# A smaller descriptor area for indirect transfers, and one more raw and one more split weight buffer, in a recurrent block with 32 experts

## The chip, the core and the metric

The kernel runs on one core of a Trainium2 chip. The metric is the device time of one launch in microseconds (us), as the median of several runs. A core has five engines with instruction queues of their own, each worked through strictly in order: PE (TensorE, matmuls; its weight loads are listed as PEld), DVE (VectorE), ACT (ScalarE), POOL (GpSimd) and SP (SyncE). They meet only through semaphores. Data moves between the large memory (HBM) and the on-chip memory (SBUF, 128 partitions) by transfers on 16 DMA engines. SP issues the plain transfers; POOL issues the indirect ones, whose rows are picked by an index, and the descriptors of those lie in SBUF.

## The reference: what is computed

One layer over 2048 tokens of width 1024: a gated linear recurrence with a short convolution, a layer norm, a mixture of 32 experts of which each token takes two, and a second layer norm. The part that matters here is the mixture. Cut down, with the names of the reference:

```
expert = g_idx[:, None] * EXPERTS_PER_GROUP + top_i      # two of 32 for each token
...
def expert_block(args):
    xb, e = args
    hdn = jax.nn.silu(xb @ w1[e]) * (xb @ w3[e])          # 1024 -> 512, twice
    return hdn @ w2[e]                                    # 512 -> 1024
...
out = jnp.einsum('tk,tkd->td', gates.astype(x.dtype), y_slots)
```

`w1`, `w3` and `w2` are float32, 32 experts with 3 matrices of 1024 x 512 numbers each: 201 MB that have to be read once, whatever the tokens choose.

## The kernel before, in words

**Two stages.** The first, up to about 740 us, is the recurrence (`Recurrence`), which routes each token as it goes. The second runs the experts one after the other in the order of a table, and behind them, sixteen tiles of 128 tokens at a time, the last layer norm.

**Weights.** PE multiplies in float16, so each float32 weight is split into a high and a low float16 half, and products take three passes. The 32 experts' weights come in 384 loads (12 for each expert: 4 of `w1`, 4 of `w3`, 4 of `w2`) of 128 x 1024 float32 numbers, 512 KB. Each passes through these steps:

- SP issues the load into a buffer `raw` (`load_raw`, L1286). A raw buffer takes 4 KB of each partition.
- ACT writes the high half (`split_hi`, L1300) into a buffer `w`, and DVE then writes the low half (`split_lo`, L1304). For a few early loads POOL does the latter (L1644) after another ACT step (L1640). With that, the raw buffer is free again.
- A buffer `w` holds both halves of two loads, 8 KB of each partition. PE reads it in the up matmuls (`up`, L1415) or the down matmuls (`down`, L1442, and L1358 for tokens beyond 128). When the last of these is done, the buffer is free.

There are `RAWS` = 6 raw buffers and `RING` = 10 buffers `w`. Two of the weights' buffers, once, lie in a place that is otherwise used by the last layer norm (`SPARE`).

**Tokens.** POOL gathers the expert's tokens (L1315, `exs<-xhl` and `rxT<-xhl`, and `sxg<-xhl` for those beyond 128), PE transposes them (L1399, L1346), ACT copies the result to `xT` (L1404, L1349). After the up matmuls come `silu` (ACT, L1420), the product (DVE, L1427) and its split (L1431 ACT, L1435 DVE). The down matmuls' result is scaled by ACT (L1448, L1365) and POOL adds it to the tokens' rows in HBM (L1307, `acc<-row` and `acc<-sxg`). The last layer norm fetches finished rows with POOL (L1315, `y<-acc`, and `w<-acc` for the last two tiles, which lie in a buffer `w`), normalizes them with DVE and ACT (L1505 to L1529) and stores them with POOL (L1307, `out<-y`, `out<-w`). The last expert's first 128 tokens skip the way through HBM: they are fetched (`row<-acc`), finished and stored (`out<-row`) in one go, and their sums are added as well (`acc<-row`).

**What sets the order.** The order on each engine is fixed when the program is built. `Plan` records every operation with its engine, an assumed duration, what it needs and which buffers it takes. `Plan.run` then plays the program once and takes, on each engine, what can start first, by due time among those that can. A buffer that isn't free holds an operation back. So the number of buffers of each kind (`slots`, here `"raw": RAWS, "w": RING` in `MOE`) goes into the order of all engines. On the chip the engines keep that order and wait on semaphores.

**Where loads stand on SP.** A first group of loads is issued while the recurrence still ends. Then the experts' order is known, and SP reads for each coming expert its number (L1573, `TENSOR_LOAD er`) and loads its list of tokens (L1387 `idx`, L1327 `sidx`): a block of six experts' lists, into which only a few weight loads are mixed.

```
r = add("raw", "SP", 0.5, load, behind=[k.early_done] + [x.op for x in regs], dma=2.91 * WQ / 2048,
        uses=[raw] + regs)
...
a = add("w_hi", "ACT", act(WQ), hi, [r], behind=[k.big_done] * spare, uses=[raw, w])
e, us, f = ("POOL", 2.3, rest_) if on_pool else ("DVE", dve(WQ), lo)
```

**SBUF.** `bacc.Bacc` sets aside a part of each partition for the descriptors of POOL's transfers; unless it is told otherwise, 16 KB.

Of the kernel before, what the change touches and what calls it, by code (L numbers as in the profile page):

```python
# [56 lines left out]
TAIL = [13, 16, 18, 19, 21, 22, 24, 25, 26, 28, 29, 30, 31, 31, 32, 32]  # L57
WQ = 1024
NQ = 4096 // WQ
RING, RAWS = 10, 6  # L60
NOV = 64
ON_POOL = range(1, 24, 3)
SPARE = (10, 11)
# [1877 lines left out]
```

## Time and profile before

| what | value |
|---|---|
| median of 3 runs | 1574.86 us (1574.77 to 1576.59) |
| time of the profiled execution | 1576.59 us |
| its span, first to last instruction | 1574.8 us |
| mean granted TensorE clock | 0.966 of full speed |
| PE busy | 1419.7 us, 90% of the span |
| DVE busy | 1200.5 us, 76% |
| ACT busy | 1079.3 us, 69% |
| POOL busy | 326.7 us, 21% |
| DMA traffic | 371.87 MB, mean 236 GB/s |

The shares are means over two stages with different limits. The rows of the profile on which an argument rests are shown in the prediction, each ahead of its use. In the rows with windows of time, the columns are the window, its length, and for each engine the busy time with the number of instructions; the last three are the granted clock, the mean busy share of the 16 DMA engines, and GB/s. In the rows of a timeline they are start, duration, engine, line, operation, `out<-in`, and in brackets the idle time ahead of it with what ended it. SPq is SP's queue, which only issues. The chain of waits follows the work that ended last back in time; its rows are start, duration and what ran or was waited for.

### The profile page before, as it was taken

The numbers are of one execution on the slowest core, as the hardware profiler recorded it, in microseconds if no ns is written. First come the engines' busy times: TensorE is split into PE (matmuls) and PEld (weight loads), VectorE is DVE, ScalarE is ACT, GpSimd is POOL, SyncE is SP. The second block draws the span as 40 slices with busy tenths as digits, with TensorE's granted clock in tenths as the row PEclk, the third lists the DMA queues.
The fourth block names the chain that finished last, engine by engine and source line by source line (L and its number), as shares of the span: only waits on it lengthen the run. The fifth ranks groups of instructions, "written<-read, shape, count | busy, mean of one in ns | idle before, by whom it ended". The sixth has DMA issues, their size and how long they took to land. (4 is left out here: it accounts for less than half of the span.)

```text
span 1574.8 us, 33932 instructions
## 1 busy us (share of the span) xinstructions
PE 1419.7 (90%) x13223; PEld 961.8 (61%) x13223; DVE 1200.5 (76%) x2118; ACT 1079.3 (69%) x1417; POOL 326.7 (21%) x382
## 2 busy tenths in 40 slices
PE   8799999999999999999788999998979789988781
PEld 3344444444444766775567788776868678767570
DVE  6799967986688757977967878876667578767784
ACT  5699545675367643775877778787677778877873
POOL 8100000000000000000543123233133133332223
PEclk9899999999999999999999999999989999999896
DMA  9476542433334433642689899999999899999994
GB/s 325 158 237 204 183 147 95 135 108 100 100 105 127 156 123 125 208 130 88 258 282 330 299 342 353 344 349 331 300 318 335 277 334 348 341 347 329 306 337 130
DMA packets 129648, 371.87 MB, mean 236 GB/s; under 512 B 28279, under 2 KB 38783, under 8 KB 129482
## 3 DMA queue, kind: packets, MB, share of 16 engines
q1 hardware_dynamic: 108554, 315.29, 56.9%
q0 software_dynamic: 20928, 54.36, 12.9%
q8 instruction: 105, 1.72, 0.4%
q14 instruction: 61, 0.50, 0.1%
HBM read 309.92 MB, written 57.53 MB: 233 GB/s over the span
## 5 line engine op out<-in xcount | busy, mean ns | idle before, releaser
L1304 DVE SCALAR_TENSOR_TENSOR w<-raw,w 128x1024 f16<-128x1024 f32 x373 | 449.2, 1233 | 125.3 <-ACT w L1300 123.2
L1300 ACT ACTIVATE w<-raw 128x1024 f16<-128x1024 f32 x380 | 389.5, 1054 | 97.9 <-DMA raw<-w 96.9
L1415 PE MATMUL h<-xT,w 128*128 128x128 f16 (+19 forms) x6528 | 421.3, 228 | 35.2 <-ACT xT L1404 13.5
L592 PE MATMUL mm<-xt,wsp 128*128 128x512 f16 (+1 forms) x2400 | 435.8, 341 | 19.0 <-ACT xt L523 6.5
L1415 PEld LDWEIGHTS <-w 128*128 128x128 f16 x6528 | 412.0, 100 | 42.6 <-DVE w L1304 19.1
L592 PEld LDWEIGHTS <-wsp 128*128 128x128 f16 x2400 | 235.8, 99 | 210.1 <-issue 16.1
L807 PE MATMUL o<-wo,y 128*128 128x512 f16 x960 | 218.5, 379 | 0.9 <-DVE wo L486 0.6
L1442 PE MATMUL o<-w,hT 128*128 128x512 f16 (+5 forms) x744 | 170.7, 384 | 9.8 <-DVE w L1304 3.4
L955 POOL DMA_INDIRECT table<-rows,dest x32 | 35.3, 1102 | 622.5 <-DVE xr L616 312.0
L807 PEld LDWEIGHTS <-y 128*128 128x128 f16 x960 | 91.8, 98 | 103.8 <-issue 1.6
L1442 PEld LDWEIGHTS <-hT 128*128 128x128 f16 (+5 forms) x768 | 81.4, 109 | 90.4 <-issue 12.4
L1307 POOL DMA_INDIRECT acc<-row,idx x32 | 61.3, 1914 | 268.7 <-ACT row L1448 233.0
L628 DVE SCALAR_TENSOR_TENSOR xc<-xr,cw,xc 128x512 f32<-128x512 f32 (+1 forms) x150 | 92.6, 640 | 2.7
L612 ACT ACTIVATE xr<-mm 128x512 f32<-128x512 f32 x40 | 23.7, 593 | 92.5 <-PE mm L592 70.3
L705 ACT ACTIVATE tg<-ri,bh 128x512 f32<-128x512 f32 (+1 forms) x100 | 58.2, 595 | 21.9 <-PE ri L700 21.1
L700 PE MATMUL ri<-xs,wg 128*128 128x512 f16 (+1 forms) x300 | 67.9, 336 | 0.3 <-ACT tg L705 0.2
L1404 ACT ACTIVATE xT<-rt 128x1024 f16<-128x1024 f16 (+5 forms) x64 | 63.9, 1002 | 4.9 <-PE rt L1399 3.9
L759 DVE TENSOR_TENSOR_SCAN th<-ta,hlast,tg 128x512 f32<-128x512 f32 (+1 forms) x50 | 52.4, 1066 | 1.4
L1448 ACT ACTIVATE row<-o,idx 128x512 f32<-128x512 f32 (+5 forms) x64 | 43.2, 677 | 14.6 <-PE o L1442 14.5
L1358 PE MATMUL o<-w,hT 128*32 128x256 f16 (+1 forms) x864 | 41.4, 307 | 13.0 <-ACT row L1448 13.0
L822 ACT ACTIVATE sd<-mv,epst 128x1 f32<-128x1 f32 x16 | 4.7, 295 | 68.1 <-DVE mv L818 57.5
L1427 DVE SCALAR_TENSOR_TENSOR hid<-h,hid 128x256 f32<-128x256 f32 (+19 forms) x68 | 30.1, 442 | 25.6 <-PE h L1415 25.4
(294 smaller groups left out, 1732.3 us busy)
## 6 DMA issues: line engine op xcount, KB each, us to landing
raw<-w SPq DMA_DIRECT2D x384, 512.0 KB
wsp<-wpre SPq DMA_DIRECT2D x80, 512.0 KB
row<-w_in SPq DMA_DIRECT2D x20, 512.0 KB
wpre<-wsp SPq DMA_DIRECT2D x20, 512.0 KB
row<-x SPq DMA_DIRECT2D x16, 512.0 KB
acc<-row SPq DMA_DIRECT2D x16, 512.0 KB
xhl<-exs SPq DMA_DIRECT2D x16, 512.0 KB
row<-w_out SPq DMA_DIRECT2D x10, 512.0 KB
```

The source lines that it names most:

```text
L592: nc.tensor.matmul(o, wt[:, a, d], x[:, b], start=(d == 0 and i == 0), stop=(d == KD - 1 and i == 2))
L628: nc.vector.scalar_tensor_tensor(xc, xr[:, t:t + N], s.cw[:, j, t:t + 1], xc, op0=OP.mult, op1=OP.add)
L700: nc.tensor.matmul(cell["ri"][j], a, b, start=(i == 0), stop=(i == len(seq) - 1))
L705: nc.scalar.activation(s.halves(c, s.tiles["t", c, js[0], g], js)[j], cell["ri"][j], AF.Tanh, scale=0.5 / WS, bias=s.bh[:, j, g:g + 1])
L759: nc.vector.tensor_tensor_scan(cut(h)[j], cut(T["a", c, q])[j], cut(t1())[j], s.hlast[:, j:j + 1], op0=OP.mult, op1=OP.add)
L807: nc.tensor.matmul(o, y[:, b, t * P:(t + 1) * P], s.wo[:, a, j, n * 512:(n + 1) * 512], start=(j == 0 and m == 0), stop=(j == NT - 1 and m ...
L1300: nc.scalar.activation(w[:, 0, o:o + WQ], raw, AF.Copy, scale=scale)
L1304: nc.vector.scalar_tensor_tensor(w[:, 1, o:o + WQ], raw, WS, w[:, 0, o:o + WQ], op0=OP.mult, op1=OP.subtract)
L1307: sc = nc.gpsimd.indirect_dma_start(out=to, out_offset=bass.IndirectOffsetOnAxis(ap=rows, axis=0), in_=y, in_offset=None, bounds_check=las ...
L1404: nc.scalar.activation(b.xT[:, a, :, :b.n], b.pt[a][:, :, :b.n], AF.Copy)
L1415: nc.tensor.matmul(ph[:, j], b.W[n, d // 4][:, a, o:o + P], b.xT[:, q, b.place[d], o0:o1], start=(d == 0 and m == 0), stop=(d == KD - 1 an ...
L1442: nc.tensor.matmul(py, k.hT[b.slot][:, a, i, :b.n], b.W["w2", i // 2][:, q, o:o + 512], start=(i == 0 and m == 0), stop=(i == KF - 1 and m ...
```

## The change

The build call gets an argument that sets the descriptors' part to 4 KB of each partition. The 12 KB that come free hold one more raw buffer (4 KB) and one more buffer `w` (8 KB).

```
-RING, RAWS = 10, 6
+RING, RAWS = 11, 7
...
-    nc = bacc.Bacc("TRN2", target_bir_lowering=False, num_devices=1)
+    nc = bacc.Bacc("TRN2", target_bir_lowering=False, num_devices=1, dynamic_dma_scratch_size=4096)
```

No instruction is added or removed, but the planner gets other numbers of buffers, and the order of all engines changes from the first weight load on. Ahead of it, in the recurrence, nothing moves. Three places.

SP, where the first weight loads stand, at the end of the recurrence (`xhl<-exs` and `acc<-row` are the recurrence's last stores):

```order
 L846 DMA xhl<-exs 128x2048
 L834 DMA acc<-row 128x1024
-L1286 DMA raw<-w 128x1024 x6
+L1286 DMA raw<-w 128x1024 x7
 L834 DMA acc<-row 128x1024
 L846 DMA xhl<-exs 128x2048
```

The first group, which needs no buffer back, is seven loads instead of six.

SP, in the block of six experts' lists. Before:

```order
L1286 DMA raw<-w 128x1024
L1327 ISA
L1327 DMA sidx<-table 128x1x4
L1573 TENSOR_LOAD er
L1573 ISA x2
L1387 ISA
L1387 DMA idx<-table 128x4
L1327 ISA
L1327 DMA sidx<-table 128x1x4
L1573 TENSOR_LOAD er
```

The same place in the change:

```order
L1286 DMA raw<-w 128x1024
L1327 ISA
L1327 DMA sidx<-table 128x1x4
L1573 TENSOR_LOAD er
L1573 ISA x2
L1387 ISA
L1387 DMA idx<-table 128x4
L1286 ISA
L1286 DMA raw<-w 128x1024
L1327 ISA
L1327 DMA sidx<-table 128x1x4
```

The first row is load 30 of before and load 31 of the change. Before, no further load stands ahead of the end of the block. In the change two more are mixed into it, so that 33 loads are issued by the end of the block where it were 30.

Behind that place the loads and splits of experts 4 to 9 stand up to five ahead of where they were, counted against the same expert's `silu` on ACT; from expert 17 on the two orders agree within two loads.

POOL, at the program's end (`row` is the last expert's tile, `w` the buffer with the last two tiles of the layer norm, `y_...` the two ahead of them; the numbers are the buffers'):

```order
 L1315 DMA row<-acc,idx 112x1024
 L1315 DMA w<-acc,tok 128x1024 x2
-L1307 DMA out<-y_20445,tok_out 2048x1024 x2
+L1307 DMA out<-y_20499,tok_out 2048x1024 x2
+L1307 DMA acc<-row,idx 2048x1024
 L1307 DMA out<-row,idx 2048x1024
-L1307 DMA out<-w,tok_out 2048x1024
-L1307 DMA acc<-row,idx 2048x1024
-L1307 DMA out<-w,tok_out 2048x1024
+L1307 DMA out<-w,tok_out 2048x1024 x2
```

The last expert's addition to HBM stood between the last two stores of the result; now it stands ahead of the last three.

## The prediction, made before the changed kernel was run

> **What bounds the kernel now.** I read the slices first, then the windows of time of the expert stage, then the waits and the chain of waits there. The slices (40 of 39.4 us each; the first row is the DMA engines' busy share in tenths):
>
> ```profile
> DMA  9476542433334433642689899999999899999994
> GB/s 325 158 237 204 183 147 95 135 108 100 100 105 127 156 123 125 208 130 88 258 282 330 299 342 353 344 349 331 300 318 335 277 334 348 341 347 329 306 337 130
> ```
>
> Up to slice 19 (750 us) the transfers have room. From slice 21 on they have hardly any. The windows say how much:
>
> ```profile
> 742.00:830.00 88.00, 71.80 (x961) 53.16 (x961) 72.58 (x159) 66.93 (x87) 39.26 (x24) 0.94 0.76 259
> 850.00:1520.00 670.00, 595.77 (x7600) 496.70 (x7601) 505.17 (x601) 510.03 (x640) 191.25 (x115) 0.96 0.97 331
> 1000.00:1100.00 100.00, 89.30 (x1167) 72.82 (x1165) 72.78 (x92) 76.62 (x99) 31.11 (x19) 0.97 1.00 350
> ```
>
> Over the 670 us from 850 to 1520 the 16 DMA engines are 97% busy, and PE is busy 596 us (89%). At a full share they move 350 GB/s. So this stage is bound by its transfers, with 3% of 670 = 20 us in which they run dry; PE is 74 us behind them, ahead of DVE and ACT. Who waits for whom, in us in total, times, and the longest:
>
> ```profile
> SPq L1286 <- DVE w L1304: 351.4, 263, 8.8
> ACT w L1300 <- DMA raw<-w: 96.9, 74, 10.0
> PE h L1415 <- DVE w L1304: 9.5, 7, 2.5
> ```
>
> SP stands 351 us in front of a weight load because the raw buffer is still held by the low split of an earlier one. That alone isn't a loss, as transfers are queued meanwhile. ACT waits 97 us for loads to land. The chain of waits goes in a circle there:
>
> ```profile
> 1390.24 10.59 DMA raw<-w
> 1400.86 1.07 ACT w L1300
> ...
> 1403.10 1.22 DVE w L1304
> 1404.35 9.99 DMA raw<-w
> 1414.36 1.06 ACT w L1300
> ```
>
> A load takes 10 to 10.6 us, mostly in the queue behind five others, then a high split of 1.07 and a low split of 1.22, and the freed buffer takes the next load. This circle of six is the place of the change.
>
> **The change part by part.** The sums are made against the profiled execution: 1576.59 us, its span 1574.8 and 1.8 around it. That execution lies 1.73 above the median of 1574.86, which I take off at the end.
>
> *Loads moved ahead: 3.* The order of SP (shown with the change) has 33 instead of 30 loads ahead of the end of the block of lists. The seventh raw buffer brings one, the eleventh buffer `w` two. In the trace that block holds the loads up:
>
> ```profile
> 816.76 0.92 SPq L1286 DMA_DIRECT2D raw<-w  x2
> 817.90 0.65 SPq L1327 DMA_DIRECT2D sidx<-table  x1
> ...
> 827.83 0.62 SPq L1327 DMA_DIRECT2D sidx<-table  x1
> 828.72 6.24 SPq L1286 DMA_DIRECT2D raw<-w  x7
> ```
>
> From 817.7 to 828.7 no load is issued, and the share between 742 and 830 is 0.76, so there is room for three more. A stage bound by transfers ends earlier by what was moved ahead of it: 3 loads of 0.524 MB at 350 GB/s, 1.50 us each, 4.5 us. The ends: nothing, if PE is what paces the stage after all, and 3 x 2.04 = 6.1 if a load's whole period counts, which is the time from the first to the last load over 383 steps:
>
> ```profile
> L1286 SPq DMA_DIRECT2D raw<-w x384: 327/333/3612, 742.7 to 1525.6; - x192
> ```
>
> I take 4.5, by the nearer row, that of the full windows.
>
> *Dry stretches.* Windows of 10 us in which the transfers run dry:
>
> ```profile
> 890.00:900.00 10.00, 10.00 (x124) 6.52 (x123) 8.62 (x11) 6.74 (x10) 3.15 (x2) 1.00 0.75 185
> 1140.00:1150.00 10.00, 2.23 (x11) 0.88 (x10) 3.06 (x5) 3.49 (x5) 0.00 (x0) 0.80 0.70 190
> 1240.00:1250.00 10.00, 6.82 (x48) 3.50 (x47) 2.77 (x3) 3.96 (x6) 0.00 (x0) 1.00 0.81 286
> 1250.00:1260.00 10.00, 5.77 (x62) 5.53 (x60) 2.88 (x5) 8.17 (x11) 2.47 (x2) 0.83 0.46 170
> 1480.00:1490.00 10.00, 7.16 (x65) 3.15 (x65) 5.26 (x6) 7.43 (x10) 2.78 (x2) 0.66 0.78 258
> ```
>
> They lack 2.5, 3.0, 1.9, 5.4 and 2.2 us, 15 of the 20. In such a stretch all loads that had a buffer have landed, and SP can't issue another. One more raw buffer puts one more load into it, 1.5 us at most: 5 x 1.5 = 7.5. Nothing shows how often the reshuffled order meets such a stretch again, so I take the middle between 0 and 7.5, 3.7 us, and keep for the range 0 and the whole 20.
>
> *The end.* The last additions and stores of POOL, and what two of them wait for:
>
> ```profile
> 1557.35 1.94 POOL L1307 DMA_INDIRECT out<-row,idx  x1 [4.94 <-DVE tsd L1528]
> 1559.59 0.97 POOL L1307 DMA_INDIRECT out<-w,tok_out  x1 [0.30 <-issue]
> 1560.86 1.57 POOL L1307 DMA_INDIRECT acc<-row,idx  x1 [0.30 <-issue]
> 1562.73 1.01 POOL L1307 DMA_INDIRECT out<-w,tok_out  x1 [0.30 <-issue]
> ```
> ```profile
> 1554.94 1.24 ACT L1448 ACTIVATE row<-o,idx 112x512 f32<-112x512 f32 x2
> 1559.77 1.28 DVE L1529 SCALAR_TENSOR_TENSOR w<-w,tsd,lnb 128x1024 f32<-128x1024 f32 x1
> ```
>
> `acc<-row` needs ACT's row, done at 1556.2, in a stretch where POOL is idle. Moved there it ends at 1557.9, and the others follow with their durations and 0.30 between them: 1558.2, 1560.4, and the last at 1561.7, behind DVE's end at 1561.05. That is 1.0 us sooner.
>
> *Nothing else is added.* ACT and DVE do the same 384 splits. The first load group of seven instead of six lies in the recurrence's last stores, and belongs to the three loads above.
>
> *The descriptors.* Each of POOL's transfers stands there with its duration (min/median/max in ns), and a dense stretch holds four issues within 8 us (first and last shown), of which the last lands after 9.87 by the chain:
>
> ```profile
> L1307 POOL DMA_INDIRECT acc<-row,idx x32: 1534/1910/2564, 806.0 to 1560.9; - x32
> L1315 POOL DMA_INDIRECT rxT<-xhl,idx x15: 942/1490/2658, 822.9 to 1421.6; - x15
> ```
> ```profile
> 1343.82 2.04 POOL L1307 DMA_INDIRECT acc<-row,idx  x1 [3.84 <-ACT row L1448]
> ...
> 1349.84 1.99 POOL L1307 DMA_INDIRECT acc<-sxg,siq  x1 [0.30 <-issue]
> ```
> ```profile
> 1349.84 9.87 DMA acc<-sxg,siq
> ```
>
> About five are in flight at once, and no issue takes over 2.7 us, so none waits for room with 16 KB. With 4 KB the trace has no row. The low end is nothing, since the same descriptors are written. The high end: if the quarter holds fewer than such a burst, its last one waits a landing, 9.87 us, once for each of 30 experts, 296 us if all of it lay on the path. I take nothing, by the nearest row, the issues without any wait. The Trainium skill's page "DMA: Bandwidth & Descriptors" (sections Terms, and SWDGE vs HWDGE vs iDMA) gives a descriptor 16 bytes and puts the rings of each direction into 16 partitions; if one partition serves one DMA engine, my estimate is 256 descriptors for each in 4 KB, against about nine for one transfer of 128 rows, so some 28 transfers would fit, and the sum stays as it is. No row here shows that capacity.
>
> Sum: 4.5 + 3.7 + 1.0 = 9.2. 1576.6 - 9.2 = 1567.4, less 1.7 for the median: **1565.7 us**.
>
> **The rivals.**
>
> *A. The lead isn't cashed: within 0.2% of before (3.1 us, about what a measurement of this kernel can tell from no change).* If PE paces the stage, with transposes and copies that stand in ACT's order, loads that arrive sooner only wait longer, and the end's 1.0 us remains: 1573.9. For it speaks that PE is at 89%, and that at the first dry window (890 to 900) PE was busy all 10 us. Against it: PE's 74 idle us, and the circle of the chain.
>
> *B. Slower: POOL's transfers land later.* A seventh load stands in the DMA engines beside each gather and each addition. If their time grows with the loads in flight, it grows by a sixth. The chain of waits by line says how much of it lies on the path:
>
> ```profile
> by line: issue 4.0%; DMA raw<-w 3.0%; DMA w<-acc,tok 1.1%; DMA y<-acc,tok 1.1%; DMA rxT<-xhl,idx 1.0%; DMA acc<-row,idx 0.9%; PE h L1415 0.8%; DVE w L1304 0.7%; ACT w L1300 0.7%; DMA acc<-sxg,siq 0.6%; PE o L1442 0.3%; POOL acc L1307 0.2%;
> ```
>
> `y<-acc`, `rxT`, `acc<-row` and `acc<-sxg` are 3.6%, 57 us; a sixth is 9.4. Without the dry stretches' gain the sum is 9.4 - 4.5 - 1.0 = 3.9 slower, 1578.8. It decides from a growth of a tenth on: 5.5 of 57. Against it stand gathers of 512 KB with and without loads around:
>
> ```profile
> 1483.67 7.12 DMA y<-acc,tok
> ...
> 1525.56 8.53 DMA y<-acc,tok
> ```
> ```profile
> 1545.07 0.97 POOL L1315 DMA_INDIRECT w<-acc,tok  x1 [0.30 <-issue]
> ```
> ```profile
> 1550.41 1.06 ACT L1516 ACTIVATE w<-w 128x1024 f32<-128x1024 f32 x1 [7.74 <-DMA w<-acc,tok]
> ```
>
> Behind the last load it takes 5.3 us, among six 7.1 and 8.5. Six loads cost some 2.5 us, a seventh perhaps 0.4, a twentieth. The skill's page "DMA: Bandwidth & Descriptors", section SWDGE vs HWDGE vs iDMA, says that POOL's transfers and SP's feed different queues in each DMA engine, which takes them in turns. By that a gather waits for its turns, not for the length of the other queue, and B would cost nothing; the trace agrees as far as 2.5 us for six loads, of 1.5 each, go.
>
> *C. The descriptors run short: far slower,* up to the 296 us above. The point is a burst that no longer fits. Only a new wait of POOL would tell; nothing speaks for it.
>
> *D. The dry stretches close wholly:* 4.5 + 20 + 1.0 = 25.5, or 27.1 with the longer period, 1547.8. This needs PE to follow.
>
> **How the numbers follow.** My forecast with D has 0.68, all of it faster by over 0.2%; A 0.18; B 0.10 and C 0.04, slower. The range reaches from 1551, which leaves out the last of D (0.05), to 1579, which takes in A and B and leaves out C and the worst of B (0.08).
>
> **What would show it.** Right, if 33 loads are issued by the end of the block of lists, at about 828; if the share between 742 and 830 rises over 0.76 and that between 850 and the last loads over 0.97; if the last load starts some 8 us before 1525.6; and if POOL's last `acc<-row` lies in the idle time ahead of `out<-row`. SP's wait for DVE's split should stay of the same order, as the circle is still bound by transfers, with about 11.5 us for a load instead of 10. For A it would show that loads land sooner but `h` starts no sooner, with more idle time of ACT and SP. For B, that the gathers' parts of the chain grow. For C, that POOL's issues take longer than 2.7 us or stand idle with no wait named. Wrong would be the whole reading if the dry stretches were longer than before: then the order of the queues, not the number of buffers, makes them.

## The result, and the profile after

| | before | after |
|---|---|---|
| median, us (6 runs each) | 1575.72 (1573.90 to 1579.03) | 1533.76 (1532.51 to 1536.88) |
| ratio after to before, 95% interval | | 0.9735 (0.9721 to 0.9749) |
| span of the profiled execution, us | 1574.8 | 1531.9 |

The change is 42 us faster, where 9 were forecast. The sign was right and the size was not; the time lies below the range.

The slices of after (38.3 us each; DMA share in tenths, then GB/s):

```profile
DMA  9476533332424443452578999999999999999995
GB/s 321 165 240 211 202 109 127 130 118 65 140 87 139 143 139 130 136 190 78 208 250 280 383 348 379 362 350 364 360 274 364 359 313 363 380 342 329 344 345 147
```

In before no slice of the expert stage is above 353 GB/s. Here eight are at 360 or more. What looked like a stage at its full rate wasn't at it. The windows of after: those of the same stretches as before, and two of 10 us (from 1130 and from 1225) in dry stretches that are left:

```profile
720.00:850.00 130.00, 111.52 (x1308) 76.45 (x1307) 102.80 (x228) 97.43 (x135) 51.48 (x31) 0.95 0.72 245
742.00:830.00 88.00, 71.02 (x869) 51.59 (x867) 70.82 (x156) 64.59 (x83) 39.78 (x24) 0.92 0.72 240
850.00:1480.00 630.00, 582.97 (x7614) 487.75 (x7612) 499.57 (x596) 503.04 (x634) 187.78 (x116) 0.97 1.01 351
890.00:900.00 10.00, 10.00 (x112) 7.33 (x110) 8.88 (x13) 7.22 (x10) 0.00 (x0) 1.00 1.04 361
1000.00:1100.00 100.00, 95.95 (x1257) 82.68 (x1257) 79.91 (x99) 81.54 (x104) 30.02 (x19) 1.00 1.02 365
1130.00:1140.00 10.00, 10.00 (x181) 7.98 (x181) 7.75 (x7) 10.00 (x14) 6.19 (x4) 0.84 0.86 249
1225.00:1235.00 10.00, 6.46 (x65) 6.45 (x66) 4.96 (x7) 6.26 (x9) 3.69 (x3) 0.66 0.76 256
```

Two of these windows of before, for comparison, and one of 10 us:

```profile
720.00:850.00 130.00, 110.73 (x1336) 77.20 (x1335) 101.43 (x227) 98.49 (x135) 51.11 (x33) 0.96 0.71 241
850.00:1480.00 630.00, 563.09 (x7285) 473.69 (x7283) 472.14 (x562) 478.58 (x600) 179.94 (x108) 0.96 0.97 332
960.00:970.00 10.00, 10.00 (x129) 6.75 (x127) 8.43 (x10) 8.78 (x11) 0.56 (x1) 1.00 1.03 411
```

A share of 1.00 isn't the end: a window of after shows 1.04, and the last row shows that before itself had reached 1.03 and 411 GB/s for 10 us. So the 0.97 of before left more than 3% open. Between 850 and 1480 after moves 351 instead of 332 GB/s, 5.7% more. The dry stretch at 890 is gone. In windows of 10 us laid end to end from 850 to 1480, the lowest share is 0.79, where in before it was 0.46.

The weight loads' row (SPq; issue times in ns, first and last start), and after's waits that answer to the three shown of before:

```profile
L1286 SPq DMA_DIRECT2D raw<-w x384: 327/333/2728, 727.1 to 1486.0; - x192
```
```profile
SPq L1286 <- DVE w L1304: 329.1, 264, 6.4
ACT w L1300 <- DMA raw<-w: 69.2, 67, 6.5
PE h L1415 <- DVE w L1304: 6.4, 7, 1.5
```

The last load starts at 1486.0 instead of 1525.6, 39.6 us sooner, and from there to the end it is 45.9 instead of 49.2 us: together the 42.9 by which the span is shorter. The time went out of the expert stage.

### The profile page after: what moved, and what is told of

It is laid out like the page before. It is cut to its first block, busy times and chain, and to the rows that moved or that the text cites. A ratio compares the mean times of both kernels' runs of the same rounds, so it can differ in the third digit from the quotient of the medians.

```text
span 1531.9 us, 33939 instructions
## 1 busy us (share of the span) xinstructions
PE 1409.3 (92%) x13223; PEld 953.3 (62%) x13223; DVE 1198.8 (78%) x2118; ACT 1072.1 (70%) x1413; POOL 323.5 (21%) x382
## 5 line engine op out<-in xcount | busy, mean ns | idle before, releaser
L1304 DVE SCALAR_TENSOR_TENSOR w<-raw,w 128x1024 f16<-128x1024 f32 x373 | 444.4, 1225 | 96.8 <-ACT w L1300 95.7
L1415 PE MATMUL h<-xT,w 128*128 128x128 f16 (+19 forms) x6528 | 412.2, 226 | 20.1 <-ACT xT L1404 7.4
L1415 PEld LDWEIGHTS <-w 128*128 128x128 f16 x6528 | 404.4, 99 | 27.4 <-issue 12.4
L1431 ACT ACTIVATE hT<-hid 128x256 f16<-128x256 f32 (+19 forms) x68 | 29.0, 428 | 30.7 <-DVE hid L1427 30.3
```

The lines of the kernel that those rows point to most:

```text
L1304: nc.vector.scalar_tensor_tensor(w[:, 1, o:o + WQ], raw, WS, w[:, 0, o:o + WQ], op0=OP.mult, op1=OP.subtract)
L1415: nc.tensor.matmul(ph[:, j], b.W[n, d // 4][:, a, o:o + P], b.xT[:, q, b.place[d], o0:o1], start=(d == 0 and m == 0), stop=(d == KD - 1 an ...
```

## The experiments

Line 60 of the kernel holds the planner's numbers, and lines 1865 and 1866 the pools' sizes. The experiments set them apart, so that an order that was made for one number of buffers runs with another. The descriptors' part is 4 KB, by the same argument as in the change, unless the run says otherwise. "Before" was run beside each group on the same chip, and the ratio is to that. The last two columns belong to the profiled execution alone: the start of its last weight load, and the time from there to its end. They tell a gain among the loads from one behind them.

| run | order made for (w, raw) | buffers w, raw | median, us | ratio to before, 95% | last load starts, us | from there to the end, us |
|---|---|---|---|---|---|---|
| before | 10, 6 | 10, 6 | 1575.72 | | 1525.6 | 49.2 |
| e1 | 10, 6 (before's) | 10, 6 | 1572.63 | 0.9987 (0.9961 to 1.0013) | 1521.8 | 45.2 |
| e2 | 10, 6 | 10, 7 | 1555.90 | 0.9892 (0.9857 to 0.9928) | 1508.9 | 45.7 |
| e3 | 10, 7 | 10, 6 | 1567.66 | 0.9981 (0.9951 to 1.0012) | 1517.0 | 42.0 |
| e4 | 10, 7 | 10, 7 | 1537.49 | 0.9787 (0.9747 to 0.9828) | 1488.2 | 45.3 |
| e5 | 10, 6 | 11, 7 | 1556.36 | 0.9877 (0.9839 to 0.9915) | 1504.3 | 47.9 |
| e6 | 10, 9 | 10, 9 | 1553.90 | 0.9864 (0.9833 to 0.9895) | 1492.1 | 58.4 |
| e7 | 10, 6 | 10, 9 | 1549.75 | 0.9838 (0.9800 to 0.9877) | 1496.2 | 48.9 |
| e8 | 10, 6, descriptors 1 KB | 10, 6 | 1576.63 | 1.0001 (0.9979 to 1.0024) | 1531.0 | 45.0 |
| e9 | 10, 7 | 10, 9 | 1532.38 | 0.9723 (0.9699 to 0.9747) | 1481.9 | 49.1 |
| e10 | 10, 6, tail later | 10, 7 | 1545.18 | 0.9813 (0.9787 to 0.9840) | 1491.4 | 52.9 |
| e11 | 10, 6, tail later | 10, 6 | 1569.53 | 0.9984 (0.9957 to 1.0011) | 1519.2 | 45.0 |
| e12 | 10, 7, tail later | 10, 9 | 1540.92 | 0.9779 (0.9737 to 0.9821) | 1486.2 | 56.2 |
| the change | 11, 7 | 11, 7 | 1533.76 | 0.9735 (0.9721 to 0.9749) | 1486.0 | 45.9 |

### The parts of the change: e1 to e5

*e1, the descriptors alone.*

```diff
-    nc = bacc.Bacc("TRN2", target_bir_lowering=False, num_devices=1)
+    nc = bacc.Bacc("TRN2", target_bir_lowering=False, num_devices=1, dynamic_dma_scratch_size=4096)
```

> Descriptors' part 4 KB, but 6 raw and 10 split buffers and the order of before. The descriptor theory (the smaller area or the shifted addresses themselves change the time of POOL's transfers): a good part of the 42 us, at or under 1560. All other theories: as before, 1575 within 3 us, with POOL's issues and the packets' times unchanged.

No difference that can be measured: what the smaller part costs or gains is under 0.4%.

*e2, the seventh raw buffer in before's order* (line 60 stays at 10, 6):

```diff
-            k.wraw = cx.enter_context(tc.tile_pool(name="raw", bufs=RAWS, reuse_waits="tile"))
+            k.wraw = cx.enter_context(tc.tile_pool(name="raw", bufs=7, reuse_waits="tile"))
```

> The order of before on all engines, 7 raw buffers, 10 split buffers. Seventh-buffer theory (the circle of raw buffers runs dry with six loads, and one more in flight fills the stretches): at least half of the gain, 1555 or less, with the DMA share from 850 to 1520 near 0.99. Order theory (the planner's new order makes the gain, above all in experts 4 to 11): 1570 to 1576. Eleventh-buffer theory: 1570 to 1576.

*e3, the order without the buffer:*

```diff
-RING, RAWS = 10, 6
+RING, RAWS = 10, 7
...
-            k.wraw = cx.enter_context(tc.tile_pool(name="raw", bufs=RAWS, reuse_waits="tile"))
+            k.wraw = cx.enter_context(tc.tile_pool(name="raw", bufs=6, reuse_waits="tile"))
```

> The order that the planner makes for 7 raw and 10 split buffers, which is that of the change but for two weight loads in the block of lists, with 6 raw and 10 split buffers on the chip. Order theory: most of the gain, 1550 or less. Seventh-buffer theory: no better than before, 1570 to 1580, since the same order then waits more on SP. Eleventh-buffer theory: 1570 to 1576.

*e4, both:*

```diff
-RING, RAWS = 10, 6
+RING, RAWS = 10, 7
```

> Planner and chip both with 7 raw and 10 split buffers. Seventh-buffer and order theories, alone or together: nearly all of the gain, 1533 to 1540. Eleventh-buffer theory (three loads ahead and a split that waits less for PE): 1560 or more.

Measured: 1555.9, 1567.7 and 1537.5 us. By the ratios the buffer alone takes off 1.1% (17 us), the order alone 0.2% with an interval that includes no change, and both together 2.1%, some 34 us. The two help each other: the order is worth next to nothing with six loads in flight, and about as much as the buffer itself with seven. No theory by itself had that: e2 falls between the ranges of the buffer and of the order, just outside the first, and e3 lies 2 us below the range of the buffer. The last loads say the same: against e1, which has before's order and buffers, they start 13 us sooner with e2, 5 with e3 and 34 with e4.

*e5, the eleventh buffer w added to e2:*

```diff
-            k.wsp = cx.enter_context(tc.tile_pool(name="w", bufs=RING, reuse_waits="tile"))
-            k.wraw = cx.enter_context(tc.tile_pool(name="raw", bufs=RAWS, reuse_waits="tile"))
+            k.wsp = cx.enter_context(tc.tile_pool(name="w", bufs=11, reuse_waits="tile"))
+            k.wraw = cx.enter_context(tc.tile_pool(name="raw", bufs=7, reuse_waits="tile"))
```

> Before's order on every engine (the planner still gets 10 and 6), with the descriptors' part at 4 KB and pools of 11 buffers w and 7 raw. It is the run with the seventh raw buffer in the old order (1555.9 us) and the eleventh buffer w added. Seventh-buffer theory (the raw buffer alone acts in a fixed order; a buffer w holds up nothing there): 1553 to 1558. Eleventh-buffer theory (the splits of the old order wait for a free w, and the eleventh lets them run further ahead, which is what the new order did for the other 18 us): 1537 to 1548. Order theory (the rest of the gain up to 1534 comes only with the new order): as the first, above 1550.

1556.4 beside e2's 1555.9: in before's order the eleventh `w` does nothing that can be measured. From e4 to the whole change are 3.7 us, and there the eleventh `w` also moves two more loads into the block of lists; the two intervals overlap.

### More buffers, fewer descriptors: e6, e7, e8

*e6, the change's memory given to raw buffers alone* (10 x 8 + 9 x 4 = 116 KB, as 11 x 8 + 7 x 4):

```diff
-RING, RAWS = 10, 6
+RING, RAWS = 10, 9
```

> The change's room given to raw buffers alone: 10 buffers w and 9 raw, in the planner too, descriptors' part 4 KB. Seven raw and ten w gave 1537.5 us with 12.8 us of dry DMA time left between the first load of the stage and the last one. Depth theory (what pays is the number of loads in flight, and two more close most of what is left dry and go on shortening the packets' time): 1522 to 1531, better than the change (1533.8). Saturation theory (seven loads cover all but the stretches that other waits make; the rest is the transfers' own rate): 1534 to 1540. Contention theory (POOL's gathers land later with nine loads beside them): above 1541.

*e7, nine raw buffers in before's order:*

```diff
-            k.wraw = cx.enter_context(tc.tile_pool(name="raw", bufs=RAWS, reuse_waits="tile"))
+            k.wraw = cx.enter_context(tc.tile_pool(name="raw", bufs=9, reuse_waits="tile"))
```

> Before's order on every engine, 10 buffers w, 9 raw, descriptors' part 4 KB. Seven raw in this order gave 1555.9 us, six gave 1572.6. Depth theory (each raw buffer goes on gaining by itself, whatever the order): 1535 to 1545. Order theory (in the old order the low splits stand behind waits for the tail's gathers, and further buffers fill as the seventh did but with falling gain): 1546 to 1553. Saturation theory: 1553 to 1558.

e7 gives 1549.8 us, 6 below e2's seven buffers, as the order theory had it, though the two intervals overlap. e6 gives 1553.9, in the range of the contention theory alone, and 16 slower than e4 with its seven: the depth theory falls, and e9 below tests the contention. One dry stretch of e6 shows a wait on DVE (timeline; in brackets the idle time ahead of it and what ended it):

```profile
1458.29 1.28 DVE L1505 BATCH_NORM_STATS2 tst<-y 128x6 f32<-128x512 f32 x2 [10.86 <-DMA y<-acc,tok]
...
1461.78 4.63 DVE L1304 SCALAR_TENSOR_TENSOR w<-raw,w 128x1024 f16<-128x1024 f32 x4
```
```profile
1450.00:1460.00 10.00, 7.14 (x116) 7.14 (x117) 1.51 (x4) 4.30 (x6) 2.83 (x3) 0.83 0.65 218
```

DVE stood 10.86 us in front of the statistics of the last layer norm, whose rows a gather of POOL had yet to bring. Behind them in its queue were four low splits, which alone release raw buffers in this stage, and the transfers ran at 0.65. But most of what e6 loses isn't lost there: by the table its last load starts 3.9 us later than e4's, and the stretch behind it is 13.1 us longer. What makes that end longer wasn't separated. The same wait, for the rows of the layer norm (the tail), is in e2, where its statistics hold up five splits, and in the deepest dry stretch of before:

```profile
1249.46 1.29 DVE L1505 BATCH_NORM_STATS2 tst<-y 128x6 f32<-128x512 f32 x2 [10.05 <-DMA y<-acc,tok]
...
1250.90 5.72 DVE L1304 SCALAR_TENSOR_TENSOR w<-raw,w 128x1024 f16<-128x1024 f32 x5
```
```profile
1258.31 1.29 DVE L1505 BATCH_NORM_STATS2 tst<-y 128x6 f32<-128x512 f32 x2 [6.97 <-DMA y<-acc,tok]
...
1259.76 5.72 DVE L1304 SCALAR_TENSOR_TENSOR w<-raw,w 128x1024 f16<-128x1024 f32 x5
```

In after a wait for the tail at nearly that time looks so:

```profile
1231.23 1.29 DVE L1505 BATCH_NORM_STATS2 tst<-y 128x6 f32<-128x512 f32 x2 [4.38 <-DMA y<-acc,tok]
...
1232.68 1.18 DVE L1304 SCALAR_TENSOR_TENSOR w<-raw,w 128x1024 f16<-128x1024 f32 x1
...
1236.36 5.76 DVE L1304 SCALAR_TENSOR_TENSOR w<-raw,w 128x1024 f16<-128x1024 f32 x5
```

The wait is shorter. The splits behind it are no fewer: one directly, and five more behind three short steps of the tail. All such waits of the stage (850 to 1500; total us, times, longest), in this order before, e2, e7, e4 and after:

```profile
DVE tst L1505 <- DMA y<-acc,tok: 15.6, 6, 7.0
```
```profile
DVE tst L1505 <- DMA y<-acc,tok: 28.9, 9, 10.1
```
```profile
DVE tst L1505 <- DMA y<-acc,tok: 30.1, 8, 10.9
```
```profile
DVE tst L1505 <- DMA y<-acc,tok: 10.9, 5, 4.5
```
```profile
DVE tst L1505 <- DMA y<-acc,tok: 12.0, 7, 4.4
```

In before's order, with more buffers, DVE waits at the statistics for twice as long. In the order of e4 and after the statistics stand where the gathers have nearly landed. That is a theory of what the order gains with seven buffers; e10 tests it. The total of this wait doesn't rank the runs by itself: it is 1.9 us in e3 with six raw buffers, 13.7 in e6, and 17.1 in e9, which is as fast as the change.

*e8, a quarter of the descriptors again:*

```diff
-    nc = bacc.Bacc("TRN2", target_bir_lowering=False, num_devices=1)
+    nc = bacc.Bacc("TRN2", target_bir_lowering=False, num_devices=1, dynamic_dma_scratch_size=1024)
```

> Before's order and buffers (10 and 6), with the descriptors' part at 1 KB, a quarter of the change's. Shows how far rival C of the prediction is away. If even a quarter holds what POOL has in flight: 1569 to 1576, as with 4 KB (1572.6). If it holds about one transfer at a time, an issue waits for the landing of the one ahead: POOL's issues of 2 us grow to up to 10, with some 30 bursts of four in the expert stage and more in the recurrence: from 1600 up to 1870.

1576.6 us, 0.6 above the expected range, and the interval of the ratio includes no change, even at 1 KB. POOL's issues there take up to 3.1 us (2.7 in before), and their medians are no longer than before's 1.9 and 1.5:

```profile
L1307 POOL DMA_INDIRECT acc<-row,idx x32: 1533/1643/3089, 809.5 to 1565.6; - x32
L1315 POOL DMA_INDIRECT rxT<-xhl,idx x15: 949/1456/2922, 828.5 to 1422.3; - x15
```

At one place, though, POOL stands idle with no wait named, which is the sign that the prediction gave for rival C. An addition and the store behind it, in e8 and then in before:

```profile
1236.75 2.33 POOL L1307 DMA_INDIRECT acc<-row,idx  x1 [7.70 <-issue]
1256.79 1.03 POOL L1307 DMA_INDIRECT out<-y,tok_out  x1 [17.72 <-issue]
```
```profile
1229.38 2.56 POOL L1307 DMA_INDIRECT acc<-row,idx  x1 [1.51 <-ACT row L1448]
1232.25 1.02 POOL L1307 DMA_INDIRECT out<-y,tok_out  x1 [0.30 <-issue]
```

With 4 KB (e1) the two stand idle for 0.45 and 0.30 us. Whether 1 KB ran short there isn't shown: before has a wait without a name too, of 7.81 us ahead of another gather. The time of the whole kernel shows no cost.

### The order by itself: e9 to e12

*e9, the order of e4 with nine raw buffers:*

```diff
-RING, RAWS = 10, 6
+RING, RAWS = 10, 7
...
-            k.wraw = cx.enter_context(tc.tile_pool(name="raw", bufs=RAWS, reuse_waits="tile"))
+            k.wraw = cx.enter_context(tc.tile_pool(name="raw", bufs=9, reuse_waits="tile"))
```

> The order of the run with 10 buffers w and 7 raw (1537.5 us) on every engine, with pools of 10 w and 9 raw, descriptors' part 4 KB: the same memory as the change. Nine raw buffers in two other orders gave 1549.8 (before's order) and 1553.9 us (the planner's own for nine). Order theory (with enough buffers the time is set by how long the order makes DVE stand in front of a gather of the tail with low splits behind it; this order has the least of that): 1526 to 1537, clearly below both. Buffer theory (nine buffers cost something, such as gathers that land later beside nine loads, whatever the order): 1545 to 1556.

1532.4 us, as the order theory had it. With the same nine buffers three orders give 1553.9, 1549.8 and 1532.4 us. So the contention theory falls: nine loads in flight cost nothing that can be measured in this order, and in before's order they gain little over seven (e7). e9 and the change can't be told apart.

*e10, e2 with the tail's statistics later.* Only the place of the tail's steps (statistics, root, scaling and store, tiles 0 to 11) in the emitted order moves; on SP nothing does.

```diff
-        for o in sorted(order, key=lambda o: (o.start, o.i)):
+        for o in sorted(order, key=lambda o: (o.start + getattr(o, "later", 0.0), o.i)):
...
-                        table="q" if e == "ACT" else None)
-        add("out", "POOL", 1.05, b.store, [o], uses=[y], dma=1.46, want=end + 25.0)
+                        table="q" if e == "ACT" else None); o.later = 8.0 * (i < BY_ACT)
+        add("out", "POOL", 1.05, b.store, [o], uses=[y], dma=1.46, want=end + 25.0).later = o.later
```

> The run with before's order and the seventh raw buffer (1555.9 us), with one thing moved: the tail's steps on DVE and ACT between a gather and its store (the first twelve tiles) stand 8 planned us later among their engine's work, so that up to six low splits pass ahead of each. SP's order and all loads stay as they were. In that run DVE waited 28.9 us in all, 9 times, 10.1 at the longest, for a gather to land, with low splits queued behind. Theory of the tail's wait (those splits hold the raw buffers, and this is what the new order mended): the wait falls under 12 us and the time to 1538 to 1549. Rival (the waits lie beside full transfers and cost nothing; the new order gains elsewhere): 1552 to 1559.

1545.2 instead of 1555.9, and the intervals of the ratios don't overlap. The wait for the tail shrinks from 28.9 us to this, and the stretch in which e2 was driest is full; e2's window is shown behind e10's:

```profile
DVE tst L1505 <- DMA y<-acc,tok: 4.7, 3, 2.5
```
```profile
1240.00:1250.00 10.00, 10.00 (x126) 9.63 (x124) 8.84 (x10) 8.02 (x10) 6.09 (x4) 1.00 1.02 315
```
```profile
1240.00:1250.00 10.00, 6.18 (x63) 6.07 (x63) 0.54 (x1) 7.13 (x8) 0.99 (x1) 0.83 0.52 173
```

So the place of twelve tiles' steps is worth 10.7 us with seven raw buffers, over half of the 18 between e2 and e4. Among the loads it is worth more: the last one starts at 1491.4 instead of 1508.9, 17.5 us sooner, where e4's starts 20.7 sooner. The stretch behind it is 7.2 us longer than e2's, so part of the gain is lost again at the end. The steps on ACT and the stores on POOL moved together with DVE's, so that the gain comes through DVE's wait is read from its row, and wasn't separated from those.

*e11, the same with six raw buffers* (e1 with the edit of e10):

> Before's order and before's buffers (10 w, 6 raw; descriptors' part 4 KB), with the tail's steps 8 planned us later as in the run before it (1545.2 us with seven raw). Tells whether the tail's wait and the seventh buffer are worth their sum or more. If each is worth the same alone (the seventh 17, the later tail 11): 1560 to 1564. If they help each other (with six loads in flight the stretches run dry for other waits as well): 1565 to 1572, near the 1567.7 of the new order with six. If the later tail is worth more with fewer loads in flight, since each wait drains them sooner: below 1559.

1569.5 us: next to nothing, as with e3, and with an interval that includes no change. The waits of DVE for transfers in the stage are these, without a single one for the tail, and then the longest of them on DVE and on SP:

```profile
DVE siq L1333 <- DMA sidx<-table: 17.6, 4, 9.8
```
```profile
1226.08 3.45 DVE L1304 SCALAR_TENSOR_TENSOR w<-raw,w 128x1024 f16<-128x1024 f32 x3
1239.32 0.16 DVE L1333 SCALAR_TENSOR_TENSOR siq<-sidx,part 128x2 int32<-128x2 int32 x1 [9.79 <-DMA sidx<-table]
```
```profile
1224.13 0.61 SPq L1327 DMA_DIRECT2D sidx<-table  x1
1225.01 24.48 SPq L1286 DMA_DIRECT2D raw<-w  x9
```

In place of the tail's wait there is one for an expert's list of tokens, at nearly the same time, with low splits behind it again. SP had issued that list at 1224.13, behind the loads that were already queued. In e10, the same order with seven raw buffers, DVE doesn't wait for a list in the stage at all. SP comes to the list only when the loads ahead of it have got their buffers, so a further buffer should bring the list out sooner; that reason is argued, not shown.

*e12, e9 with the edit of e10:*

> The order of the change without its eleventh buffer w, 10 w and 9 raw (1532.4 us), with the tail's steps 8 planned us later. There DVE still waited 17.1 us, 4 times, 8.2 at the longest, for a gather of the tail, with some 12 us of dry transfers left in the stage. Theory of the tail's wait: part of those 12 us goes, 1522 to 1529, the best of all. If what is left dry has other causes (the order of PE, the additions of POOL): 1530 to 1535. If the later stores hold up the tail's buffers and so POOL: above 1536.

Slower than e9, 1540.9 against 1532.4, although DVE's wait for the tail fell from 17.1 to 7.4 us. POOL's wait for the scaled rows it has to store, in e9 and then in e12, nearly doubles:

```profile
POOL out L1307 <- DVE y L1529: 34.1, 7, 9.6
```
```profile
POOL out L1307 <- DVE y L1529: 65.2, 8, 17.8
```

POOL works in order too, and its gathers and additions stand behind those stores. So the tail can stand too late as well as too early. By the table 4.3 us are lost ahead of the last load and 7.1 behind it. How much is due to this wait wasn't separated.

## Why the prediction was right and wrong, by its own steps

- **What bounds the stage: right.** The loads' circle is the place of the change, and one more buffer in it alone gave 17 us (e2). PE was not the bound: between 850 and 1480 it is busy 583 instead of 563 us, doing the same work sooner. Rival A falls.
- **"At a full share they move 350 GB/s", and 20 us missing: wrong.** The ceiling was taken from a window of before that was itself held back. After shows 365 GB/s over the same 100 us, and before's own window from 960 to 970 shows 1.03 and 411. From the windows 850 to 1480: the share rises from 0.97 to 1.01, 4.1%, and what a full share moves from 332/0.97 = 342 to 351/1.01 = 348 GB/s, 1.5%. On the 675.6 us from 850 to the last load of before that is some 27 and 10 us, as far as shares with two digits tell. The first alone is more than the 20 that were to be had at most; the second wasn't in the sum, nor in rival D.
- **"Dry stretches", 3.7: the step that failed.** It was sized as one load for each of five stretches, halved, with 20 at most. Of the 42.9 us by which the span is shorter some 38 belong here, as the other two terms below make 1.5 and at most 3.3. A seventh buffer does not add 1.5 us to each of five: in before's order it gives 17 us (e2). And the stretches were put down to the number of loads alone, while in the deepest of them DVE waits for something else, with the splits that release the buffers queued behind. That stands in before's timeline at 1258, and the prediction doesn't use it. A better order shortens those waits, and only with the seventh buffer does that pay (e3 and e11 against e4 and e10). The prediction treated order and buffer as one term, and as luck of the order what the two make together.
- **"Loads moved ahead", 4.5: too large.** The two loads stand in the block of lists, and 33 are issued by its end, as foreseen, though that end is at 833 and not at 828:

```profile
818.45 1.02 SPq L1286 DMA_DIRECT2D raw<-w  x2
819.69 0.66 SPq L1327 DMA_DIRECT2D sidx<-table  x1
821.65 0.35 SPq L1387 DMA_DIRECT2D idx<-table  x1
822.27 0.75 SPq L1286 DMA_DIRECT2D raw<-w  x1
824.64 0.64 SPq L1327 DMA_DIRECT2D sidx<-table  x1
826.64 0.34 SPq L1286 DMA_DIRECT2D raw<-w  x1
```

  The share between 742 and 830 didn't rise, it fell from 0.76 to 0.72, because the first group moved out of that window: its first load starts at 727.1 instead of 742.7. From 720 to 850 the mean goes from 241 to 245 GB/s; 4 GB/s x 130 us = 0.52 MB, about one load and not three. That is 1.5 us.
- **"The end", 1.0: right in place.** The last `acc<-row` stands in POOL's idle time ahead of `out<-row`:

```profile
1517.02 2.05 POOL L1307 DMA_INDIRECT acc<-row,idx  x1 [3.03 <-ACT row L1448]
1519.38 0.95 POOL L1307 DMA_INDIRECT out<-row,idx  x1 [0.30 <-DVE tsd L1528]
1520.91 1.79 POOL L1307 DMA_INDIRECT out<-w,tok_out  x1 [0.58 <-DVE w L1529]
```

  The stretch behind the last load is 3.3 us shorter; what of it is this step wasn't separated.
- **Descriptors, 0: right** for 4 KB (e1), and rival C falls; how much room is left is less sure, by the two idle times of e8. By the Trainium skill's page "DMA: Bandwidth & Descriptors" (sections Terms, and SWDGE vs HWDGE vs iDMA) the estimate made ahead of the run for 4 KB comes for 1 KB to 64 descriptors and some seven transfers. Five were in flight in before, and e8's time agrees with that estimate; its two idle times aren't explained by it, as POOL had issued only two transfers in the 25 us ahead of the first.
- **Rival B: no cost of it.** From issue to landing `rxT` takes 10.5 us in the median instead of 9.2 and `acc<-sxg` 9.4 instead of 8.6, while `y<-acc` (7.7, was 7.6) and `acc<-row` (9.4, was 9.7) stay. Nine loads beside POOL's transfers give 1532.4 us (e9). **Rival D, the dry stretches close wholly,** was the nearest, and fell short for the reason in the second point: 27.1 us for all, against 42 measured.

What stays open: the 8 us between the medians of e10 and e4, whose intervals overlap (in the profiled executions 3.2 us lie ahead of the last load and 7.6 behind it, and PE's order differs too); why e6 and e12 have so long an end; and why a full share moves 1.5% more. Over 1000 to 1100 e2 moves 347 GB/s and e7 349, with seven and nine loads in before's order, and e4 365: more loads in flight alone don't bring it, and no run isolates it.

## What to carry to other kernels

Don't take a long window with a share of 1.00 for the ceiling of a stage that works in a circle of buffers: it has been measured with the circle's own limit, shorter windows can show more, and the dry time counted against it is a lower bound. When transfers run dry, look on the engine that releases the buffers for what stands ahead of the releasing instruction, and what that waits for; a further buffer and a better place for that instruction may each be worth little and together a lot. And an order belongs to the number of buffers for which it was made: when a planner makes a new one, try the old and the new order with each number before crediting the buffer.

## What the runs showed of the hardware that was not expected

- The mean busy share of the 16 DMA engines goes over 1.00: to 1.03 in 10 us of before, with 411 GB/s, and to 1.04 in 10 us of after. A slice of 38 us of after moved 383 GB/s, where the best of before's moved 353.
- With a descriptors' part of 4 KB this kernel takes 0.9987 (0.9961 to 1.0013) of the time with 16 KB, and with 1 KB 1.0001 (0.9979 to 1.0024), there with one place where POOL stands idle for 7.70 and 17.72 us without a named wait.
- A list of tokens (128 x 4 numbers), issued by SP at 1224.13 behind 512 KB loads, was awaited by DVE until 1239.32, 15 us after its issue, for 9.79 us of idle time (e11).
